# Two-layer attention trunk: layer 0's 256-column head products and layer 1's rotary ones as three float32r products, a new order of the first loads, and one place for layer 0's weight halves

## The chip, the cores and the metric

The kernel runs on one core of one Trainium2 chip. The metric is the device time of one execution in microseconds (us), the median of several runs. TensorE (PE in the profile) multiplies, PEld is its loading of stationary operands, VectorE is DVE, ScalarE is ACT, GpSimd is POOL, and SyncE (SP) issues most transfers.

## The reference

One sequence of 256 tokens with 2048 features in float32 goes through two layers. Each layer adds to x an attention and then a gated feed-forward, both behind an RMS norm. Cut to what matters:

```python
# layer 0: 16 heads of 128; with 256 tokens there is one key block, so this is causal attention
q = rope(rms_norm((h @ wq).reshape(B, S, H, dh), gq), pos, rot)      # rot = 32
k = rope(rms_norm((h @ wk).reshape(B, S, H, dh), gk), pos, rot)
v = (h @ wv).reshape(B, S, H, dh)
p = softmax(where(causal, einsum('bqhd,bhkd->bhqk', q, k) * dh ** -0.5, NEG_INF))
y = einsum('bhqk,bhkd->bqhd', p, v).reshape(B, S, H * dh) @ wo
# layer 1: low-rank q and kv; a rotary key of 64 columns is shared by the 16 heads
s = (einsum('bqhd,bkhd->bhqk', qn, k_nope) + einsum('bqhr,bkr->bhqk', qr, k_rope)) * scale
y = einsum('bhqk,bkhd->bqhd', softmax(where(causal, s, NEG_INF)), v).reshape(B, S, H * VD) @ wo
# feed-forward of each layer, 5632 wide
y = (silu(conv3(h @ w_gate) + b) * (h @ w_up)) @ w_down
```

## The kernel before, in words

**The stream of weights.** All weights pass through the core once, 370 units of up to 1 MB, cut into 1480 pieces of 128 x 512 (some 128 x 288). `Stream.load` (L72) issues a unit's transfer on SyncE's queue; three units are on their way at a time. `Stream.split` makes two float32r tiles of each piece: `whi`, a copy by ScalarE (L100), and `wlo`, the rest by VectorE (L101). It runs up to four pieces ahead of TensorE (one at the start, more by and by: `min(1 + q // 6, AHEAD_PIECES)`). A float32 product x·w becomes three float32r products: high·high, high·low, low·high.

**Two kinds of piece.** `tok_major` (L234 to L236) holds 128 tokens of h as the stationary operand and moves 512 columns of the piece: six products a piece, three for each half of the tokens. `feat_major` (L251 to L253) holds 128 columns of the piece and moves 256 tokens: twelve products a piece. Each of the two tiles of a piece has 64 spare columns, and `starts` says at which column it begins, one value for `whi` and one for `wlo`. Layer 0's q, k and v weights are units 0 to 47, twelve for each of four groups of four heads; `BY_HEADS` gives each group a place of its own, (8, 8), (8, 40), (56, 24) and (24, 56). Other token-major pieces use `BY_TOKEN` = (8, 8), feature-major ones `BY_FEATURE` = (24, 56).

**What sets the order.** The program is a list of quanta, one for a weight piece. `add` appends the products of a piece, `at(q, f)` puts other work behind quantum q, `first(q, f)` ahead of it. The last loop issues for each quantum: work put ahead, `ws.split` up to four pieces on, the products, the work behind. Each engine works strictly in the order in which its instructions were issued, and waits for others by semaphores. So the weight halves of later pieces stand on VectorE and ScalarE behind the heads' work of earlier quanta.

**The heads.** In layer 0, group g takes 48 pieces: 16 each for q, k and v. `Heads` takes q or k of four heads from PSUM (L364), sums squares (L369), asks GpSimd for the power -1/2 (L382), scales (L395), rotates (L425 to L430, through `ro1`, `ro2`), and lets TensorE transpose two heads at a time (L439); ScalarE copies the result to `qT` or `kT` (L447). `evac_values` (L549) copies v. `plan_heads` puts these at q + 0 to q + 10. A `Head` then makes the scores of 128 queries against 128 keys and of the other 128 against 256 (L463; in layer 1 a rotary product follows each, L466), masks them and takes maxima (L473), exponentiates (L482), normalises (L489, L491), transposes three blocks (L499), copies them to `pT` (L504), multiplies with v (L510 with 256 columns, L511 with 128), and splits the result into `oT` (L517 high, L518 low). All of these products are plain float32. A float32 and a float32r matmul both read f32 in the profile's rows; the line tells them apart.

**Layer 1's shared key.** `kva_turn` and `kva_rotate` prepare it, `kr_turn` (behind quantum q + 9 of the last kv piece) transposes it (L819), GpSimd clears two tiles of `room` (L823), and VectorE copies 64 rows into each (L824): the tile for even heads has the upper rows filled, the one for odd heads the lower ones.

**The way in.** TensorE runs nine products of zeros (L173). SyncE issues alternately a quarter of each of the first units (L84) and one or more of the 16 blocks of x (L177); ScalarE's queue issues the first part of `par` (L176), which holds the norm's gains. `Norm.high` (L269, ScalarE) and `Norm.low` (L274, VectorE) make a block of h, and the first piece is cast and split behind them.

Of the kernel before, what the change touches and what calls it, by code (L numbers as in the profile page):

```python
# [10 lines left out]
F32 = mybir.dt.float32  # L11
# [6 lines left out]
P = 128  # L18
# [31 lines left out]
BY_HEADS = ((8, 8), (8, 40), (56, 24), (24, 56))  # L50
# [4 lines left out]
class Stream:  # L55
# [20 lines left out]
    def begin(self, load_x):  # L76

        ends = (1, 2, 3, 4, 6, 6, 8, 8, 10, 10, 13, 16)
        at = 0
        for u in range(AHEAD_UNITS):  # L80
            src, k, n = self.units[u]
            self.raw[u] = t = self.raw_pool.tile([P, 4 * 512], F32, name="raw")
            for i in range(k):
                self.nc.sync.dma_start(t[:, i * n : (i + 1) * n], src[:, i * n : (i + 1) * n])  # L84
                end = ends[u * k + i]
                if end > at:
                    load_x(at, end)
                    at = end
        self.loaded = AHEAD_UNITS

    def split(self, upto):
        while self.split_to < min(upto, len(self.pieces)):
# [7 lines left out]
            self.nc.scalar.copy(hi[:, :n], w)  # L100
# [11 lines left out]
def trunk(ctx: ExitStack, tc: tile.TileContext, a, out):  # L112
# [39 lines left out]
    def starts(u, j):  # L152

        if u < 48:
            return BY_HEADS[u // 12]
        return BY_TOKEN if 200 <= u < 222 else BY_FEATURE
# [15 lines left out]
    for _ in range(9):  # L172
        mm(idle, zeros[:, :P], zeros, start=True, stop=True)  # L173
    warm = const.tile([P, 1], F32, name="warm")
    nc.scalar.activation(warm, ones, AF.Square)
    nc.scalar.dma_start(par[:, :C_CW], a["par"][:, :C_CW])  # L176
# [48 lines left out]
    def tok_major(state, lhs, kt, k_last, t_hi, t_lo, n):  # L225
# [4 lines left out]
        for t in range(NT):  # L230
            hi = src[:, kt, t * P : (t + 1) * P]
            lo = src[:, kt, S + t * P : S + (t + 1) * P]
            o = state["acc"][t][:, :n]
            mm(o, hi, t_hi[:, :n], start=kt == 0, stop=False)  # L234
            mm(o, hi, t_lo[:, :n], start=False, stop=False)  # L235
            mm(o, lo, t_hi[:, :n], start=False, stop=kt == k_last)  # L236
# [106 lines left out]
    class Heads:  # L343
# [22 lines left out]
        def squares(self, t):  # L366
            for i in range(self.n):
                junk = att_pool.tile([P, P], F32, name="junk", bufs=2)
# [38 lines left out]
        def rotate(self, t, stages=(0, 1)):  # L407
# [11 lines left out]
            def part(name):  # L419
                r = att_pool.tile([P, 16 * 32], F32, name=name, bufs=2)  # L420
# [30 lines left out]


    class Head:
        def __init__(self, h, qT, kT, v, i, oT, scale, rope=None):
            self.h, self.qT, self.kT, self.v, self.i = h, qT, kT, v, i
            self.oT, self.scale, self.rope = oT, scale, rope

        def scores(self):
            sc = ps_sc.tile([P, 512], F32, name="sc")
            qT, kT, i = self.qT(), self.kT(), self.i  # L460
            for q0, n, c in ((0, P, 0), (P, S, P)):
                o = sc[:, c : c + n]
                mm(o, qT[:, i, q0 : q0 + P], kT[:, i, :n], start=True, stop=self.rope is None)  # L463
                if self.rope is not None:
                    qr, kr = self.rope()
                    mm(o, qr[:, q0 : q0 + P], kr[:, :n], start=False, stop=True)  # L466
# [35 lines left out]
        def turned(self):  # L502
            self.pT = att_pool.tile([P, 3 * P], F32, name="pT", bufs=2)
            nc.scalar.copy(self.pT, self.tp[:, : 3 * P])  # L504

        def values(self):
# [3 lines left out]
            mm(o[:, :S], v[:, 0, vs], self.pT[:, :S], start=True, stop=False)  # L510
            mm(o[:, P:S], v[:, 1, vs], self.pT[:, S:], start=False, stop=True)  # L511
# [24 lines left out]
    def moba_tiles(g):  # L536
        if g == 0:
            env["oT"] = att_pool.tile([P, H, 2 * S], F32R, name="oT", bufs=1)
        env["qT", g] = att_pool.tile([P, 4, S], F32, name="qT")
        env["kT", g] = att_pool.tile([P, 4, S], F32, name="kT")  # L540
        env["v", g] = att_pool.tile([P, NT, 512], F32, name="v")
# [9 lines left out]
    def plan_heads(q, hs, key, step):  # L551
# [8 lines left out]
        for i0 in (0, 2):  # L560
            pair = {}
            at(q + step * 9 + i0 // 2, lambda hs=hs, p=pair, i0=i0, key=key: hs.turned(env[key], p, i0))
            at(q + step * 9 + i0 // 2,
               lambda hs=hs, p=pair, i0=i0, key=key: hs.turned_out(env[key], p, i0))
# [3 lines left out]
    for g in range(4):  # L568
        for kind in "qkv":
            state = {}  # L570
# [12 lines left out]
            if kind == "v":  # L583
                at(q, evac_values, state, ("v", g), lambda: n1.rstd)
                q_v = q
            else:
                hs = Heads(state, 4, P, G_Q if kind == "q" else G_K, 32, (tab, T_MC, T_MS), lambda: n1.rstd)
                plan_heads(q + (0 if g else 15 if kind == "q" else 9), hs, ("qT" if kind == "q" else "kT", g), 1)
                q_k = q
        for i in range(4):  # L590
            hd = Head(
                4 * g + i, lambda g=g: env["qT", g], lambda g=g: env["kT", g], lambda g=g: env["v", g],
                i, lambda: env["oT"], MOBA_SCALE,
# [152 lines left out]
    def open_mla():  # L746
# [7 lines left out]
        env["qrT"] = att_pool.tile([P, 8, S], F32, name="qrT", bufs=1)  # L754
# [9 lines left out]
    def kva_stats():  # L764
        ss = small.tile([P, NT, 2], F32, name="kvss")
        for t in range(NT):
            for k, (lo, hi) in enumerate(((0, 512), (512, 576))):
                junk = att_pool.tile([P, 512], F32, name="kvjunk", tag="ro1", bufs=2)
# [323 lines left out]
```

## Time and profile before

| | us |
|---|---|
| median of 3 runs | 2102.42 (2102.33 to 2102.92) |
| profiled execution | 2103.16 |
| its span, first to last instruction | 2101.3 |
| TensorE busy in the span | 2093.2 |
| VectorE busy | 1389.1 |
| ScalarE busy | 1135.1 |

Layer 0's projections and heads take the first 310 us or so of the span, layer 1's the stretch from some 1120 to 1320 us; the rest are output projections and feed-forwards.

How to read the lines of the profile that follow. A timeline row has the start and the length in us, the engine, the line of the program, the operation, output tile <- input tiles, shape, and xN for N of the same in a row; in square brackets stands how long the engine was idle ahead of it and what ended that. A row of groups has the count, then busy time in us and the mean in ns, then idle time. A row of waits has who waited, for whom, the total in us, how often, and the longest. The lengths of matmuls are modelled and overlap; the distance between starts is what counts.

### The profile page before, as it was taken

How to read it: one execution, taken by the hardware profiler on the slowest of the kernel's cores; microseconds unless marked ns; L12 is line 12 of the kernel's file. 1: busy time of each engine (PE TensorE's matmuls, PEld its weight loads, DVE VectorE, ACT ScalarE, POOL GpSimd, SP SyncE). 2: the span in 40 equal slices, each digit the busy share in tenths (PEclk: the TensorE clock that was granted, in tenths of full speed). 3: DMA queues.
4: the chain of work that ended last, by engine and by line, in shares of the span. 5: the costliest groups of instructions: out<-in, count | busy, mean ns of one | idle time of the engine just before them, and what ended most of it. 6: DMA issues, size and time to landing. Idle time of an engine off the chain costs nothing.

```text
span 2101.3 us, 42062 instructions
## 1 busy us (share of the span) xinstructions
PE 2093.2 (100%) x16683; PEld 2016.4 (96%) x16683; DVE 1389.1 (66%) x3035; ACT 1135.1 (54%) x2207; POOL 45.6 (2%) x37
## 2 busy tenths in 40 slices
PE   9999999999999999999999999999999999999999
PEld 7888889999999999999999889999999999999999
DVE  6766666766667666655555786767666667665554
ACT  6555555655555555555455675655555555544443
POOL 0000000000000000000000110000000000000000
PEclk9999999999999999999999999999999999999999
DMA  7444445555555555555554533555555555555553
GB/s 272 161 161 180 160 163 187 193 201 190 192 201 187 195 201 186 197 200 186 198 200 150 181 136 107 194 187 193 190 199 192 192 199 191 192 205 206 195 207 131
DMA packets 59381, 391.81 MB, mean 186 GB/s; under 512 B 6960, under 2 KB 10032, under 8 KB 13232
## 3 DMA queue, kind: packets, MB, share of 16 engines
q1 hardware_dynamic: 59040, 389.10, 52.1%
q8 instruction: 130, 2.13, 0.4%
q14 instruction: 67, 0.55, 0.1%
q10 hardware_dynamic: 144, 0.04, 0.0%
HBM read 387.01 MB, written 2.10 MB: 185 GB/s over the span
## 4 chain that ended last, share of the span: by engine, by line
PE 98%; DVE 1%; issue 0%; ACT 0%; POOL 0%; DMA 0%; SPq 0%; POOLq 0%; ACTq 0%
PE acc L251 26%; PE acc L253 26%; PE acc L252 26%; PE acc L235 5%; PE acc L234 5%; PE acc L236 5%; PE sc L463 1%; PE tp L439 1%; PE sc L510 1%; PE tp L499 0%; PE sc L466 0%; PE sc L511 0%; DVE wlo L101 0%; DVE junk L369 0%; POOL hr L382 0%
## 5 line engine op out<-in xcount | busy, mean ns | idle before, releaser
L101 DVE TENSOR_TENSOR wlo<-raw,whi 128x512 fp32r<-128x512 f32 (+1 forms) x1480 | 1000.8, 684 | 426.6 <-ACT whi L100 424.8
L100 ACT CAST whi<-raw 128x512 fp32r<-128x512 f32 (+1 forms) x1480 | 872.8, 614 | 463.7 <-PE acc L252 213.8
L251 PE MATMUL acc<-h,whi 128*128 128x256 f32 x2880 | 795.3, 276 | 0.0
L253 PE MATMUL acc<-h,wlo 128*128 128x256 f32 x2880 | 794.9, 276 | 0.0
L252 PE MATMUL acc<-h,whi 128*128 128x256 f32 x2880 | 794.9, 276 | 0.0
L252 PEld LDWEIGHTS acc<-h,whi 128*128 128x128 f32 x2880 | 540.7, 188 | 0.0
L251 PEld LDWEIGHTS acc<-h,whi 128*128 128x128 f32 x2880 | 540.7, 188 | 0.0
L253 PEld LDWEIGHTS acc<-h,wlo 128*128 128x128 f32 x2880 | 540.6, 188 | 0.0
L251 PE MATMUL acc<-a,whi 128*128 128x256 f32 x1408 | 388.6, 276 | 0.0
L252 PE MATMUL acc<-a,whi 128*128 128x256 f32 x1408 | 388.6, 276 | 0.0
L253 PE MATMUL acc<-a,wlo 128*128 128x256 f32 x1408 | 388.6, 276 | 0.0
L251 PEld LDWEIGHTS acc<-a,whi 128*128 128x128 f32 x1408 | 264.3, 188 | 0.0
L252 PEld LDWEIGHTS acc<-a,whi 128*128 128x128 f32 x1408 | 264.3, 188 | 0.0
L253 PEld LDWEIGHTS acc<-a,wlo 128*128 128x128 f32 x1408 | 264.3, 188 | 0.0
L234 PE MATMUL acc<-whi,h 128*128 128x512 f32 (+1 forms) x448 | 177.0, 395 | 0.7 <-ACT whi L100 0.7
L235 PE MATMUL acc<-wlo,h 128*128 128x512 f32 (+1 forms) x448 | 170.8, 381 | 0.1
L236 PE MATMUL acc<-whi,h 128*128 128x512 f32 (+1 forms) x448 | 170.2, 380 | 0.0
L251 PE MATMUL acc<-oT,whi 128*128 128x256 f32 x512 | 144.9, 283 | 0.0
L253 PE MATMUL acc<-oT,wlo 128*128 128x256 f32 x512 | 141.7, 277 | 0.0
L252 PE MATMUL acc<-oT,whi 128*128 128x256 f32 x512 | 141.6, 277 | 0.0
L665 DVE TENSOR_TENSOR g<-acc,rstd_b 128x256 f32<-128x256 f32 x88 | 37.5, 426 | 126.0 <-PE acc L253 123.0
L672 ACT ACTIVATE c<-g,par 128x256 f32<-128x256 f32 x88 | 53.1, 603 | 107.8 <-DVE g L665 107.8
(146 smaller groups left out, 1739.1 us busy)
## 6 DMA issues: line engine op xcount, KB each, us to landing
raw<-in_ffn_gu SPq DMA_DIRECT2D x176, 1024.0 KB, 4.8
raw<-in_ffn_down SPq DMA_DIRECT2D x88, 1024.0 KB, 4.8
raw<-in_moba_wk SPq DMA_DIRECT2D x16, 1024.0 KB, 4.9
raw<-in_moba_wv SPq DMA_DIRECT2D x16, 1024.0 KB, 4.8
raw<-in_moba_wo SPq DMA_DIRECT2D x16, 1024.0 KB, 4.8
raw<-in_mla_wo SPq DMA_DIRECT2D x16, 1024.0 KB, 4.8
raw<-in_moba_wq SPq DMA_DIRECT2D x13, 1024.0 KB, 4.8
raw<-in_mla_wkv_a SPq DMA_DIRECT2D x8, 576.0 KB, 3.9
```

Source lines behind the costliest of these rows:

```text
L100: self.nc.scalar.copy(hi[:, :n], w)
L101: self.nc.vector.tensor_tensor(lo[:, :n], w, hi[:, :n].bitcast(F32), op=ALU.subtract)
L234: mm(o, hi, t_hi[:, :n], start=kt == 0, stop=False)
L235: mm(o, hi, t_lo[:, :n], start=False, stop=False)
L236: mm(o, lo, t_hi[:, :n], start=False, stop=kt == k_last)
L251: mm(o, w_hi, src[:, kt, :S], start=first and k == 0, stop=False, skip_group_check=True)
L252: mm(o, w_hi, src[:, kt, S:], start=False, stop=False, skip_group_check=True)
L253: mm(o, w_lo, src[:, kt, :S], start=False, stop=kt == k_last, skip_group_check=True)
L439: nc.tensor.transpose(tp[:, (i * NT + t) * P : (i * NT + t + 1) * P], flat[:, t, c : c + P], ident)
L463: mm(o, qT[:, i, q0 : q0 + P], kT[:, i, :n], start=True, stop=self.rope is None)
L665: nc.vector.tensor_tensor(self.g[:, 2:], self.gate["acc"][:, :S], self.norm.rstd_b, op=ALU.mult)
L672: nc.scalar.activation(self.c, self.g[:, 2:], AF.Identity, bias=par[:, cb : cb + 1], scale=self.cw(2))
```

## The change

1. `Head.scores` and `Head.values` of layer 0, and the rotary part of layer 1's scores, make each product of 256 columns as three float32r products (`three`). The products of 128 columns stay float32, and so does layer 1's 256-column product of the unrotated parts.
2. For that, operands get a high and a low part. `queries_out` and `keys_out` take the place of one ScalarE copy: a float32r high part (ScalarE), a float32 copy of the first 128 columns (ScalarE), and the low part (VectorE). `evac_parts` does so for v, `Head.turned` for the transposed map. The tiles for q and k of layer 0 have one buffer instead of two. `kr_turn` writes a high and a low part and a float32 copy, and fills the other rows of the first two with zeros by VectorE.
3. `junk`, `ro1`, `ro2` and `kvjunk` have one buffer instead of two.
4. `BY_HEADS` goes: layer 0's q, k and v pieces all begin at (8, 8).
5. The way in: `par` and the first block of x go out first on SyncE's queue, the first weight quarter on ScalarE's; VectorE casts the first piece, which is split ahead of the first block of h; ten products of zeros instead of nine; the first piece's six products run in the order high·high for both token halves, then high·low, then low·high.

```diff
-BY_HEADS = ((8, 8), (8, 40), (56, 24), (24, 56))
...
-        ends = (1, 2, 3, 4, 6, 6, 8, 8, 10, 10, 13, 16)
-        at = 0
+        ends = (2, 2, 3, 4, 6, 6, 8, 8, 10, 10, 13, 16)
+        load_x(0, 1)
+        at = 1
...
-                self.nc.sync.dma_start(t[:, i * n : (i + 1) * n], src[:, i * n : (i + 1) * n])
+                queue = self.nc.scalar if u == i == 0 else self.nc.sync
+                queue.dma_start(t[:, i * n : (i + 1) * n], src[:, i * n : (i + 1) * n])
...
-            self.nc.scalar.copy(hi[:, :n], w)
+            if i == 0:
+                self.nc.vector.tensor_copy(hi[:, :n], w)
+            else:
+                self.nc.scalar.copy(hi[:, :n], w)
...
-        if u < 48:
-            return BY_HEADS[u // 12]
-        return BY_TOKEN if 200 <= u < 222 else BY_FEATURE
+        return BY_TOKEN if u < 48 or 200 <= u < 222 else BY_FEATURE
...
-    for _ in range(9):
+    for _ in range(10):
...
-    nc.scalar.dma_start(par[:, :C_CW], a["par"][:, :C_CW])
+    nc.sync.dma_start(par[:, :C_CW], a["par"][:, :C_CW])
...
+        if state.get("first") and kt == 0:
+            order = [(t, part) for part in range(3) for t in range(NT)]
+        else:
+            order = [(t, part) for t in range(NT) for part in range(3)]
...
+    def three(o, w_hi, w_lo, m_hi, m_lo, start, stop):
+        mm(o, w_hi, m_hi, start=start, stop=False)
+        mm(o, w_hi, m_lo, start=False, stop=False)
+        mm(o, w_lo, m_hi, start=False, stop=stop)
...
+            if self.parts:
+                (q0, q1), (k0, k) = qT, kT
+                mm(sc[:, :P], q0[:, i], k0[:, i], start=True, stop=True)
+                three(sc[:, P : 3 * P], q1[:, 0, i], q1[:, 1, i], k[:, 0, i], k[:, 1, i], True, True)
+            else:
+                qr0, qr1, kr0, kr = self.rope()
+                mm(sc[:, :P], qT[:, i, :P], kT[:, i, :P], start=True, stop=False)
+                mm(sc[:, :P], qr0, kr0, start=False, stop=True)
+                mm(sc[:, P : 3 * P], qT[:, i, P:], kT[:, i], start=True, stop=False)
+                three(sc[:, P : 3 * P], qr1[:, 0], qr1[:, 1], kr[:, 0], kr[:, 1], False, True)
...
+            nc.scalar.copy(hi, self.tp[:, :S])
+            nc.scalar.copy(self.pT1, self.tp[:, S : 3 * P])
+            nc.vector.tensor_tensor(lo, self.tp[:, :S], hi.bitcast(F32), op=ALU.subtract)
...
+                three(o[:, :S], v0[:, 0, vs], v0[:, 1, vs], self.pT[:, 0], self.pT[:, 1], True, False)
+                mm(o[:, P:S], v1[:, vs], self.pT1, start=False, stop=True)
...
+    def keys_out(dst, tp, i0):
+        k0, k = dst
+        src = tp.rearrange("p (a s) -> p a s", a=2)
+        hi, lo = k[:, 0, i0 : i0 + 2], k[:, 1, i0 : i0 + 2]
+        nc.scalar.copy(hi, src)
+        nc.scalar.copy(k0[:, i0 : i0 + 2], src[:, :, :P])
+        nc.vector.tensor_tensor(lo, src, hi.bitcast(F32), op=ALU.subtract)
...
         for i in range(2):
-            nc.gpsimd.memset(env["kr"][i], 0.0)
-            nc.vector.tensor_copy(env["kr"][i][i * 64 : (i + 1) * 64, :], tp[i * 64 : (i + 1) * 64, :S])
+            rows, rest = (slice(j * 64, (j + 1) * 64) for j in (i, 1 - i))
+            hi, lo = env["kr"][:, i, 0], env["kr"][:, i, 1]
+            nc.gpsimd.memset(env["kr0"][:, i], 0.0)
+            for t in (hi, lo):
+                nc.vector.tensor_copy(t[rest], zeros[rest, :S])
+            nc.vector.tensor_copy(hi[rows], tp[rows, :S])
+            nc.vector.tensor_tensor(lo[rows], tp[rows, :S], hi[rows].bitcast(F32), op=ALU.subtract)
+            nc.vector.tensor_copy(env["kr0"][rows, i], tp[rows, :P])
...
+    ws.split(1)
     for f, args in side.pop(-1):
```

`queries_out` is `keys_out` with the token halves the other way round (the high and low parts of the second 128 queries, a float32 copy of the first), and `evac_parts` splits v's first 128 tokens and copies the rest.

110 lines of the change are left out of this document (73 added, 37 removed).

## The prediction

> **What bounds the kernel now.** First the page: shares of the engines and the chain that ended last.
>
> ```profile
> PE 2093.2 (100%) x16683; PEld 2016.4 (96%) x16683; DVE 1389.1 (66%) x3035; ACT 1135.1 (54%) x2207; POOL 45.6 (2%) x37
> PE 98%; DVE 1%; issue 0%; ACT 0%; POOL 0%; DMA 0%; SPq 0%; POOLq 0%; ACTq 0%
> ```
>
> TensorE is 98% of that chain, so a nanosecond taken from one of its products is a nanosecond off the span, and work on another engine counts only where TensorE then waits. Where it does, the view of who waited for whom says; asked for TensorE's matmul row from 60 to 330 us (layer 0's heads; one line is the whole answer) and from 1130 to 1340 us (layer 1's heads).
>
> ```profile
> PE tp L439 <- DVE qk L430: 0.4, 1, 0.4
> ...
> PE acc L235 <- DVE wlo L101: 0.8, 1, 0.8
> ```
>
> Layer 0 has one wait of 0.4 us. The line from layer 1, where a weight piece's low half comes late from VectorE, stands at a place that the change touches.
>
> **The change, part by part. (1) Products of 256 columns.** The groups by line and shape give the counts, the timeline the starts. A busy time of a matmul is modelled and overlaps the next, so I use the distance from one start to the next.
>
> ```profile
> L463 PE MATMUL sc<-kT,qT 128*128 128x256 f32 x32 | 9.6, 380 | 0.0
> L510 PE MATMUL sc<-pT,v 128*128 128x256 f32 x32 | 9.5, 378 | 0.0
> L466 PE MATMUL sc<-room,qrT 128*128 128x256 f32 x32 | 9.5, 379 | 0.0
> ...
> 94.27 0.59 PE L510 MATMUL sc<-pT,v 128*128 128x256 f32 x2
> 94.70 0.38 PE L511 MATMUL sc<-pT,v 128*128 128x128 f32 x2
> ...
> 1202.63 0.60 PE L463 MATMUL sc<-room 128*128 128x256 f32 x2
> 1203.07 0.59 PE L466 MATMUL sc<-room,qrT 128*128 128x256 f32 x2
> ...
> 499.78 0.28 PE L252 MATMUL acc<-h,whi 128*128 128x256 f32 x1
> ...
> 500.46 0.28 PE L252 MATMUL acc<-h,whi 128*128 128x256 f32 x1
> ```
>
> A full float32 product leaves two records, so the 32 records of each of the first three rows are 16 products, 48 in all. One takes 94.70 - 94.27 = 0.43 us, or 1203.07 - 1202.63 = 0.44. A float32r product of 256 columns takes (500.46 - 499.78) / 6 = 0.113 us in the feed-forward (the second start is the sixth after the first), three of them 0.34. There the two operands lie at other places than the heads' tiles will; layer 0's 512-column float32r products, quoted in part 2, start 0.227 apart or, at another place, 0.233; half of these are 0.113 and 0.117. I take 0.116, that is 0.348 for three against 0.435: 0.087 saved, times 48 = **4.2 us saved**. Ends: at 0.113, 4.6; at 0.122, twice the spread above it, 3.3. The 128-column products stay float32 and cost what they did.
>
> **(2) One place for layer 0's heads.** A weight piece is six products of 512 columns, so the starts of L234 six products apart give a piece. Here are pieces with nothing put between, one each from groups 0, 1, 2 and 3.
>
> ```profile
> 53.64 0.39 PE L234 MATMUL acc<-whi,h 128*128 128x512 f32 x1
> ...
> 55.00 0.39 PE L234 MATMUL acc<-whi,h 128*128 128x512 f32 x1
> ...
> 131.52 0.40 PE L234 MATMUL acc<-whi,h 128*128 128x512 f32 x1
> ...
> 132.92 0.40 PE L234 MATMUL acc<-whi,h 128*128 128x512 f32 x1
> ...
> 198.27 0.40 PE L234 MATMUL acc<-whi,h 128*128 128x512 f32 x1
> ...
> 199.66 0.39 PE L234 MATMUL acc<-whi,h 128*128 128x512 f32 x1
> ...
> 273.06 0.39 PE L234 MATMUL acc<-whi,h 128*128 128x512 f32 x1
> ...
> 274.44 0.39 PE L234 MATMUL acc<-whi,h 128*128 128x512 f32 x1
> ```
>
> Group 0, which lies where all four will lie, needs 1.36 us; groups 1, 2 and 3 need 1.40, 1.39 and 1.38. VectorE and ScalarE do the same kind of work beside all of them (squares of heads in each), so the place is what differs. The tiles that these products read keep their addresses in the change. Pieces next to transposes or a head's products are irregular in every group and I count no gain there: by the planned places that leaves about 20 quiet pieces of 48 in group 1 and 27 each in groups 2 and 3. 20 x 0.04 + 27 x 0.03 + 27 x 0.02 = 2.15; the rounding of the starts leaves 1.2 to 2.6. **2.0 us saved.**
>
> **(3) The way in.**
>
> ```profile
> 1.19 4.02 PE L173 MATMUL sc<-zeros 128*128 128x512 bf16 x9 [1.19 <-DVE zeros L170]
> 4.81 0.51 ACT L269 ACTIVATE h<-xT,par 128x256 fp32r<-128x256 f32 x1 [2.58 <-DMA xT<-in_xT]
> 5.22 0.60 ACT L100 CAST whi<-raw 128x512 fp32r<-128x512 f32 x1
> 5.86 0.69 DVE L101 TENSOR_TENSOR wlo<-raw,whi 128x512 fp32r<-128x512 f32 x1
> 5.88 0.79 PE L234 MATMUL acc<-whi,h 128*128 128x512 f32 x1 [0.67 <-ACT whi L100]
> 6.61 0.79 PE L235 MATMUL acc<-wlo,h 128*128 128x512 f32 x1
> ...
> 9.18 0.69 DVE L101 TENSOR_TENSOR wlo<-raw,whi 128x512 fp32r<-128x512 f32 x1
> ...
> 9.76 0.63 PE L236 MATMUL acc<-whi,h 128*128 128x512 f32 x1
> 10.18 0.46 PE L234 MATMUL acc<-whi,h 128*128 128x512 f32 x1
> ...
> 10.95 0.40 PE L234 MATMUL acc<-whi,h 128*128 128x512 f32 x1
> ...
> 5.00:10.00 5.00, 4.33 (x10) 1.00 0.98 307
> ```
>
> ScalarE makes h and then the weight's high half, one after the other, and TensorE, out of warm-up products, waits for the second until 5.88; then again for the low half. In the change VectorE casts the first piece while ScalarE makes h. The x transfer goes out second on SyncE's queue as before (the parameters take the weight's place ahead of it, and the weight theirs on ScalarE's queue), so I leave h at 4.81 to 5.32. The weight, issued with the first transfers as before, should come with x, at 4.8; VectorE's cast takes at most what its subtraction of that width takes, 0.69, so the high half is ready by 5.5 and the low half by 6.2. The ten warm-up products end at 1.19 + 10 x 0.427 = 5.46, and the first real one follows them. Its new order (both high-high products, then both high-low) needs the low half only at 6.3, so the gap at 6.6 goes too.
>
> Until about 10.2 a product takes 10.18 - 9.76 = 0.42 (0.427 over the stretch), and 0.227 later. TensorE's clock is slow at first, though the granted clock in the last row above (TensorE's busy time with its count, clock, share of the DMA engines, GB/s) reads 1.00 for 5 to 10 us. If the slow time still ends at 10.2, (10.18 - 5.46) / 0.427 = 11 products stand before that point instead of 9: two of 0.227, 0.46 saved. But the slow time held for 3.6 us of unbroken products from 6.6 on; with nothing broken since 1.19 it probably ends earlier, and an end at 8.6 already puts five more products ahead: 1.2. The third piece bounds it: its low half is ready at 9.18 + 0.69 = 9.87, transfers of x setting that pace, and TensorE uses it at 10.95 + 0.23, so no more than 1.3 can be had. **1.2 us saved**, ends 0.4 and 1.3. The Trainium skill, "TensorE: Matmul & The Clock Gate", Part 1, says that the array is throttled by default and is released at the end of a whole busy window of about 3.4 us that runs free of the kernel. By that rule the window that ended at 10.2 was the first whole one, and the one that ended at 6.8 was broken by the gap ahead of 5.88; unbroken, it would end the slow time at 6.8 and save the full 1.3. The trace agrees as far as one end of a slow stretch can show it.
>
> **(4) The shared rotary key of layer 1.** Here the change costs. In `kr_turn`, two copies by VectorE become ten operations.
>
> ```profile
> L491 DVE TENSOR_SCALAR s<-s,sst 128x256 f32<-128x256 f32 x32 | 11.1, 348 | 0.0
> L518 DVE TENSOR_TENSOR oT<-sc,oT 128x256 fp32r<-128x256 f32 x32 | 13.6, 424 | 27.0 <-ACT oT L517 27.0
> ...
> 1187.58 0.86 DVE L824 COPY room<-tp 64x256 f32<-64x256 f32 x2 [1.18 <-POOL room L823]
> ...
> 1189.91 0.69 DVE L101 TENSOR_TENSOR wlo<-raw,whi 128x512 fp32r<-128x512 f32 x1
> ...
> 1190.65 0.50 PE L235 MATMUL acc<-wlo,cqT 128*128 128x512 f32 x1 [0.81 <-DVE wlo L101]
> ```
>
> VectorE is free from 1187.58 - 1.18 = 1186.40 but waits for GpSimd's memset; the two copies then take 0.86, and a low half at 1189.91 ends just before the product that waited 0.81 for it. After the change VectorE starts at 1186.40 with copies of zeros, which wait for nothing. Two zero copies (0.35 by L491, of which some 0.08 overlaps the next, as three low halves of 0.69 take 1.89 in part 5: 0.27), the high part 0.43 as in L824, the low part 0.42 as in L518, and an estimated 0.29 for the copy of 128 columns, a third under L824's: 1.68, twice 3.36, to 1189.76, where it was 1188.44 before. TensorE waits at that very point, so **1.3 us is lost**. Zero copies at 0.10 or at the 0.43 of L824 make 0.6 to 1.9.
>
> **(5) What lies beside TensorE.** Layer 0 gives VectorE a low part for every q and k pair, for v and for each head's turned map: per group 2 x 0.42 + 2 x 0.69 + 0.69 + 4 x 0.42 = 4.6 us of some 70 (0.42 by L518, 0.69 by L101), and ScalarE a second, smaller copy beside each. VectorE is at 66% and runs four pieces (5.4 us) ahead of TensorE.
>
> ```profile
> L504 ACT COPY pT<-tp 128x384 f32<-128x384 f32 x32 | 15.3, 479 | 5.0 <-PE tp L499 4.9
> ...
> 140.51 1.89 DVE L101 TENSOR_TENSOR wlo<-raw,whi 128x512 fp32r<-128x512 f32 x3
> 143.10 0.69 DVE L101 TENSOR_TENSOR wlo<-raw,whi 128x512 fp32r<-128x512 f32 x1 [0.69 <-ACT whi L100]
> ```
>
> Even after a group's heaviest stretch it idles again within three low halves. A new low part waits for three transposes (0.33, an estimate) and ScalarE's copy (under the 0.48 of L504), with its own 0.42 some 1.2 us, with weight halves behind it that are wanted three pieces (4.1 us) later: hidden. Where that cover is thinnest, at the 0.4 us wait of group 0, ScalarE's extra copy adds some 0.2; ends 0 and 0.6. The single buffers for q, k, junk and the rotary parts are rewritten only after their last reader by the plan, or by the same engine: nothing. Layer 1's low parts of rotary queries (four of 0.42) fall where VectorE is ahead: nothing, 0.4 if not.
>
> **Sum:** -4.2 - 2.0 - 1.2 + 1.3 + 0.2 = **-5.9 us.** The profiled execution took 2103.16 (span 2101.3, 1.9 around it), which gives 2097.3. It lies 0.7 above the median of the three runs, 2102.42, in which the change is to be seen: **2096.5**.
>
> **The rivals.** *The place does not carry over:* the locked pace of group 0 belongs to its quiet, and with heads at work all groups run at 1.40. Part 2 turns into a loss of some 0.8 in groups 2 and 3: 2099.3. Against it: group 0's pieces with squares beside them keep 1.36. *Three products cost what one did:* with both operands of the heads' products at one place each takes 0.145 instead of 0.116: no gain in part 1, 2100.7. Against it, 512 columns take 0.227 at that same place. *VectorE holds TensorE up* (slower than before): it works in order, and every one of layer 0's 16 heads now makes it wait in mid-queue for TensorE and ScalarE. If its lead there were under about 1.8 us (1.2 of waiting and a low half of 0.60), TensorE would wait some 1.1 us a head: 17.6 - 5.9 = 11.7 lost, 2114.1. Against it: no such wait in the view today, though low parts of the heads' outputs already wait in the same way. *The slow clock ends when it did:* 2097.2, inside the forecast.
>
> **How the numbers follow.** Forecast with either end of the slow clock 0.82; place 0.07; products 0.05; VectorE 0.06. The forecast's own terms reach from -4.6 - 2.6 - 1.3 + 0.6 = -7.9 to -3.3 - 1.2 - 0.4 + 1.9 + 1.0 = -2.0, not all at once; I state 2094.5 to 2100.2, which takes in the rival of the place. A run can tell about 0.2%, 4.2 us, from no change: faster means below 2098.2. Of the forecast's 0.82, 0.75 lies there and 0.07 above; the place gives 0.02 and 0.05; the products 0.05 to no change; VectorE 0.06 to slower. Faster 0.77, same 0.17, slower 0.06.
>
> **What would show it.** Right: the heads' three products start 0.113 to 0.12 apart; pieces of groups 1 to 3 with nothing between take 1.36; the first real product starts near 5.5 and fast ones well before 10.2; the wait for the low half near 1190 us grows from 0.8 to some 2.1 us. Wrong: VectorE's low halves as the releaser of waits in layer 0, pieces of 1.38 or more in groups 1 to 3, or another lasting wait in layer 1.

## The result and the profile after

The changed kernel takes **2107.35 us** (median of 11 runs, 2106.47 to 2108.44); the kernel before took 2102.92 beside it (11 runs, 2102.16 to 2103.77). The ratio is 1.0021 (95% interval 1.0012 to 1.0029): 4.4 us slower, where 2096.5 was forecast. The span of the profiled execution is 2105.5 us, 4.2 over that of before.

The page after, busy shares and the chain that ended last:

```profile
PE 2089.8 (99%) x16732; PEld 2013.4 (96%) x16732; DVE 1418.3 (67%) x3084; ACT 1137.8 (54%) x2242; POOL 45.3 (2%) x37
PE 92%; DVE 5%; ACT 1%; issue 1%; DMA 1%; POOL 1%; SPq 0%; ACTq 0%; POOLq 0%
```

TensorE is busy 3.4 us less, so products and place did act. But its share of the chain fell from 98 to 92%, and VectorE's rose from 1 to 5%: the end now runs through VectorE at many places. Who waited for whom on TensorE, first from 60 to 330 us (layer 0's heads), then from 1130 to 1340 us (layer 1's):

```profile
PE tp L449 <- DVE qk L440: 0.9, 2, 0.4
PE acc L235 <- DVE wlo L105: 0.5, 1, 0.5
```

```profile
PE acc L235 <- DVE wlo L105: 5.1, 5, 2.3
PE tp L885 <- DVE ckv L862: 1.4, 2, 1.2
PE tp L898 <- DVE krr L880: 1.1, 2, 0.7
```

Each kernel has line numbers of its own: L449 is the transpose of q and k (L439 before), L105 the low half (L101), L885 and L898 the transposes of layer 1's compressed values and of its shared key (L806 and L819). In layer 1 one wait of 0.8 for a low half has become five of 5.1 together, and not only at `kr_turn`.

To see where the time went, I set the start of each weight piece's first product beside the same piece of before. After minus before, in us, with the time in the kernel before: +0.56 at piece 18 (33 us), +1.30 at 40 (64 us), +2.07 at 50 (79 us), then falling through layer 0 to -0.72 at piece 204 (325 us), flat through the feed-forward, -0.72 still at 809, then up to +4.8 at 878 (1251 us), from where layer 1's heads bring it down to the +4.2 of the end. So the products and the place did gain, and three stretches took it back: the first pieces, group 0's first heads, and layer 1's preparation (a fourth, within groups 1 to 3, shows only beside an experiment). The trace says by what. VectorE sums squares in between, and here is the first set of them, before (L369) and after (L379):

```profile
53.37 0.28 DVE L369 CUSTOM_DVE_ANT_0 junk<-qk 128x128 f32<-128x128 f32 x1
53.59 0.08 DVE L369 DVE_READ_ACCUMULATOR2_ANT ss<- 128x1 f32 x1
53.59 0.28 DVE L369 CUSTOM_DVE_ANT_0 junk<-qk 128x128 f32<-128x128 f32 x1
...
54.01 0.28 DVE L369 CUSTOM_DVE_ANT_0 junk<-qk 128x128 f32<-128x128 f32 x1
```

```profile
53.94 0.29 DVE L379 CUSTOM_DVE_ANT_0 junk<-qk 128x128 f32<-128x128 f32 x1
54.15 0.08 DVE L379 DVE_READ_ACCUMULATOR2_ANT ss<- 128x1 f32 x1
54.27 0.29 DVE L379 CUSTOM_DVE_ANT_0 junk<-qk 128x128 f32<-128x128 f32 x1
...
54.94 0.29 DVE L379 CUSTOM_DVE_ANT_0 junk<-qk 128x128 f32<-128x128 f32 x1
```

Before, a square starts with the reading of the last one's accumulator: 0.21 us from start to start. After, 0.12 us pass between the reading's start and the next square: 0.33 us. In the program as built, each square now waits on VectorE's own semaphore until the square just before it has written `junk`; with two buffers it waits for the one before that, which is long done. The reading of the accumulator belongs to the square: the next one starts 0.04 us after the reading's end (54.15 + 0.08 against 54.27). There are 160 squares, in runs of four to eight, so some 120 such gaps, about 14 us of VectorE's time. 128 of the 160 are those of q and k (`junk<-qk`), which TensorE wants next.

The rows that answer to the other steps. The three products of 256 columns (L464 to L466) start 0.11 to 0.12 apart, as forecast, except that in the scores the first stands 0.20 ahead of the second; one set of scores and of values:

```profile
84.46 0.36 PE L464 MATMUL sc<-k,q 128*128 128x256 f32 x1
84.66 0.28 PE L465 MATMUL sc<-k,q 128*128 128x256 f32 x1
84.78 0.28 PE L466 MATMUL sc<-k,q 128*128 128x256 f32 x1
84.90 0.40 PE L235 MATMUL acc<-whi,h 128*128 128x512 f32 x1
...
95.97 0.28 PE L464 MATMUL sc<-pT,v 128*128 128x256 f32 x1
96.08 0.28 PE L465 MATMUL sc<-pT,v 128*128 128x256 f32 x1
96.20 0.28 PE L466 MATMUL sc<-pT,v 128*128 128x256 f32 x1
```

Pieces of groups 1, 2 and 3 with nothing between (the products with the low half stand three apart, so twice the distance is a piece): 0.68, 1.36 a piece in all three.

```profile
127.15 0.39 PE L235 MATMUL acc<-wlo,h 128*128 128x512 f32 x1
...
127.83 0.39 PE L235 MATMUL acc<-wlo,h 128*128 128x512 f32 x1
...
198.10 0.39 PE L235 MATMUL acc<-wlo,h 128*128 128x512 f32 x1
...
198.78 0.39 PE L235 MATMUL acc<-wlo,h 128*128 128x512 f32 x1
...
274.47 0.39 PE L235 MATMUL acc<-wlo,h 128*128 128x512 f32 x1
...
275.15 0.39 PE L235 MATMUL acc<-wlo,h 128*128 128x512 f32 x1
```

The way in: the first real product starts at 5.25, products stand 0.23 apart from 5.84 on (a row with x2 or x3 holds two or three), and then TensorE waits, for the second piece's low half and the third piece's high half, behind x's third block at 8.37.

```profile
5.25 0.75 PE L235 MATMUL acc<-whi,h 128*128 128x512 f32 x2
5.84 0.63 PE L235 MATMUL acc<-wlo,h 128*128 128x512 f32 x2
6.30 1.02 PE L235 MATMUL acc<-whi,h 128*128 128x512 f32 x3
...
7.54 0.50 PE L235 MATMUL acc<-wlo,h 128*128 128x512 f32 x1 [0.22 <-DVE wlo L105]
...
8.37 0.51 ACT L279 ACTIVATE h<-xT,par 128x256 fp32r<-128x256 f32 x1 [1.60 <-DMA xT<-in_xT]
...
9.44 0.50 PE L235 MATMUL acc<-whi,h 128*128 128x512 f32 x1 [0.47 <-ACT whi L104]
```

### The profile page after: what moved, and what is told of

Same layout as the page of the kernel before. It is cut to its first block, busy times and chain, and to the rows that moved or that the text cites. A ratio compares the mean times of both kernels' runs of the same rounds, so it can differ in the third digit from the quotient of the medians.

```text
span 2105.5 us, 42253 instructions
## 1 busy us (share of the span) xinstructions
PE 2089.8 (99%) x16732; PEld 2013.4 (96%) x16732; DVE 1418.3 (67%) x3084; ACT 1137.8 (54%) x2242; POOL 45.3 (2%) x37
## 4 chain that ended last, share of the span: by engine, by line
PE 92%; DVE 5%; ACT 1%; issue 1%; DMA 1%; POOL 1%; SPq 0%; ACTq 0%; POOLq 0%
PE acc L263 26%; PE acc L261 26%; PE acc L262 26%; PE acc L235 11%; DVE wlo L105 1%; DVE junk L379 1%; DVE qk L405 1%; PE tp L449 1%; POOL hr L392 1%; PE tp L520 0%; ACT whi L104 0%; DMA raw<-in_moba_wq 0%; ACT qk L374 0%; PE sc L545 0%; DMA xT<-in_xT 0%
## 5 line engine op out<-in xcount | busy, mean ns | idle before, releaser
L105 DVE TENSOR_TENSOR wlo<-raw,whi 128x512 fp32r<-128x512 f32 (+1 forms) x1480 | 1000.3, 684 | 402.1 <-ACT whi L104 399.2
L235 PE MATMUL acc<-whi,h 128*128 128x512 f32 (+1 forms) x896 | 277.4, 382 | 0.5 <-ACT whi L104 0.5
L235 PEld LDWEIGHTS acc<-whi,h 128*128 128x128 f32 x896 | 164.7, 188 | 30.9 <-ACT whi L104 1.4
```

Of the source, the lines that this page charges most:

```text
L105: self.nc.vector.tensor_tensor(lo[:, :n], w, hi[:, :n].bitcast(F32), op=ALU.subtract)
L235: mm(state["acc"][t][:, :n], src[:, kt, c : c + P], (t_lo if part == 1 else t_hi)[:, :n], start=kt == 0 and part == 0, stop=kt == k_last a ...
```

## The experiments

The theory: the single buffer of `junk` holds VectorE up, and VectorE's lead at q, k and the low halves behind them was thin. The rival: VectorE's new low parts and `kr_turn` hold it up. Medians below are over 6 to 11 runs unless said, each beside the kernel before on the same chip (2102.63 to 2103.00).

| kernel | median, us | ratio to before, 95% interval |
|---|---|---|
| a_junk2 | 2098.95 | 0.9981 (0.9972 to 0.9990) |
| b_junk1 | 2109.75 | 1.0032 (1.0020 to 1.0044) |
| a_oldway_j2 | 2098.14 | 0.9978 (0.9969 to 0.9987) |
| b_wayin | 2103.14 | 1.0000 (0.9991 to 1.0009) |
| b_place | 2100.34 | 0.9988 (0.9979 to 0.9997) |
| best | 2096.61 | 0.9971 (0.9960 to 0.9981) |
| b_halfx | 2102.04 | 0.9997 (0.9988 to 1.0006) |
| b_way_halfx | 2102.23 | 0.9997 (0.9988 to 1.0006) |
| b_way_dma | 2103.17 | 1.0002 (0.9993 to 1.0011) |
| b_way_comp | 2103.00 | 0.9999 (0.9990 to 1.0008) |
| best_comp | 2096.53 | 0.9970 (0.9958 to 0.9981) |
| b_ro1 | 2103.32 | 1.0002 (0.9993 to 1.0011) |
| a_products | 2100.92 | 0.9993 (0.9984 to 1.0001) |
| a_junk2_look (1 run) | 2098.29 | |
| b_u3 | 2102.38 | 0.9999 (0.9990 to 1.0008) |
| best_comp_u3 | 2096.38 | 0.9969 (0.9958 to 0.9981) |

### The one buffer

**a_junk2**, the changed kernel with this edit, and **b_junk1**, the kernel before with its reverse:

```diff
-                junk = att_pool.tile([P, P], F32, name="junk", bufs=1)
+                junk = att_pool.tile([P, P], F32, name="junk", bufs=2)
```

> The changed kernel with two buffers for the squares' output (junk) instead of one; nothing else differs. Theory A, the single buffer: the accumulating squares on VectorE now start 0.33 us apart instead of 0.21, so every set of heads leaves VectorE 0.4 to 1.6 us later, and TensorE waits for it at the transposes of the keys and at the low halves near 135, 1147, 1150 and 1253 us. With two buffers the pitch is 0.21 again and most of these waits go: about 5 us less than the changed kernel, 2102.4 (2100.5 to 2104). Theory B, the added work itself (low parts on VectorE, second copies on ScalarE, ten operations in kr_turn): the pitch returns to 0.21 but the waits stay, since VectorE's added operations cause them: 2106 to 2107.4. If the pitch stays at 0.33, the buffer is not what sets it.

> The kernel before with one buffer for the squares' output instead of two; nothing else differs. Theory A: the pitch of the squares goes from 0.21 to 0.33 us, and as VectorE was just in time at the transposes of the keys, at the two low halves behind layer 1's first rotary set and at the shared rotary key, TensorE waits there: 3 to 5 us more than before, 2105.5 to 2108. Theory B: VectorE has slack without the added work and absorbs the gaps: within 0.7 us of before.

Measured: 2098.95, which is **8.4 us under the changed kernel**, and 2109.75, 6.8 us over before; both lie beyond the ranges that I gave, on the side of theory A. This one digit is the whole loss and more. (In six of the eleven runs of a_junk2 the mean granted clock is a little under full, for which see the last section; the median of the other five is 2097.83.) The groups of squares, changed kernel first, then a_junk2 (busy and mean, then idle ahead):

```profile
L379 DVE CUSTOM_DVE_ANT_0 junk<-qk 128x128 f32<-128x128 f32 x128 | 37.1, 290 | 3.3
```

```profile
L379 DVE CUSTOM_DVE_ANT_0 junk<-qk 128x128 f32<-128x128 f32 x128 | 29.5, 286 | 0.0
```

And TensorE's waits in layer 1 in a_junk2; from 60 to 330 us only the 0.4 for L440 is left, as before the change:

```profile
PE acc L235 <- DVE wlo L105: 1.9, 1, 1.9
PE tp L885 <- DVE ckv L862: 1.4, 2, 1.2
PE tp L898 <- DVE krr L880: 0.3, 1, 0.3
```

The rival falls as the cause of the loss: with all the added low parts in place, layer 0 has no wait that it did not have. What is left of it is `kr_turn`, the wait of 1.9 us (below). The loss is larger in the changed kernel (8.4) than in the one before (6.8). The piece starts show where: groups 1 to 3 give 2.3 us between a_junk2 and the changed kernel and 0.9 between before and b_junk1. The low parts alone cost nothing there; that they use up slack in which the gaps could have hidden fits, but was not tried by itself.

**b_ro1** tests the other single buffers (`ro1`, `ro2`, and `kvjunk`, which shares the place of `ro1`) in the kernel before:

```diff
-                r = att_pool.tile([P, 16 * 32], F32, name=name, bufs=2)
+                r = att_pool.tile([P, 16 * 32], F32, name=name, bufs=1)
-                junk = att_pool.tile([P, 512], F32, name="kvjunk", tag="ro1", bufs=2)
+                junk = att_pool.tile([P, 512], F32, name="kvjunk", tag="ro1", bufs=1)
```

> The kernel before with one buffer for the rotary parts and the squares of layer 1's compressed values (which share their place), and two for junk as before. The prediction put this at nothing. The trace of the kernel with two junk buffers still has a step of 0.45 us near 1176 us, where TensorE waits for the compressed values, and none at the rotary steps: 0.3 to 0.6 above before, 2103.3. Rival: the single rotary parts hold VectorE up as the squares do, in every set of heads: 1.5 or more above before.

Measured: 0.36 over before, inside the interval of no change. The piece starts show one step of 0.37 us near 1176 us, where TensorE's wait for the compressed values (`ckv`) grows, and nothing at the rotations, where other instructions stand between a buffer's last reader and its next writer. That wait, before and in b_ro1:

```profile
PE tp L806 <- DVE ckv L783: 1.0, 2, 0.8
```

```profile
PE tp L806 <- DVE ckv L783: 1.3, 2, 1.1
```

### The place and the products

**b_place**, the kernel before with this edit alone:

```diff
-        if u < 48:
-            return BY_HEADS[u // 12]
-        return BY_TOKEN if 200 <= u < 222 else BY_FEATURE
+        return BY_TOKEN if u < 48 or 200 <= u < 222 else BY_FEATURE
```

> The kernel before with one place for layer 0's heads alone. As predicted, the quiet pieces of groups 1 to 3 fall to 1.36 us: 2.0 us saved (1.2 to 2.6), 2101.0. The trace with two buffers gives 5.1 us for layer 0 together, of which the products' measured 0.154 us a head times 16 make 2.5, so that the place would be the upper end, 2.6: 2100.4. Rival: the two do not add (the place helps only beside the new products): within 0.5 of before.

Measured: 2100.34, 2.5 us saved. **a_products** is a_oldway_j2 (below) with that edit undone, so that of the three gains only the products are left:

> The changed kernel with two buffers for the squares' output, the old way in and the old four places of layer 0's heads: the new products alone are left, with kr_turn and the single rotary buffers that came with them. If the terms add: products 3.6 us by the traces' 78, 76 and 72 ns a head and stage, less 1.1 for kr_turn and 0.4 for the rotary buffers, 2.1 below before, 2100.8 (2100.3 to 2101.3). If the place carries part of the products' gain (layer 0's operands at one place), less than 1.5 below before.

Measured: 2100.92, 1.7 us under before (2102.63), within the range expected, though its interval just takes in no change. Its piece starts gain 2.55 us in layer 0's heads and 1.3 in layer 1's. From the product ahead of a head's products to the second one behind them, the changed kernel needs 79 ns less than before in layer 0's scores, 79 in its values and 74 in layer 1's scores (means over the heads), 16 x 232 = 3.7 us. Place and products add: -2.5 and -1.7 make -4.2, and a_oldway_j2, which has both, stands 4.9 under before.

### The shared rotary key

**best** is the changed kernel with two `junk` buffers, the old way in, and a lighter `kr_turn` (the added lines stand in `open_mla`):

```diff
-            nc.gpsimd.memset(env["kr0"][:, i], 0.0)
-            for t in (hi, lo):
-                nc.vector.tensor_copy(t[rest], zeros[rest, :S])
...
-            nc.vector.tensor_copy(env["kr0"][rows, i], tp[rows, :P])
+            nc.scalar.copy(env["kr0"][rows, i], tp[rows, :P])
...
+        nc.gpsimd.memset(env["kr0"], 0.0)
+        for i in range(2):
+            for t in range(2):
+                nc.gpsimd.tensor_copy(env["kr"][(1 - i) * 64 : (2 - i) * 64, i, t], zeros[(1 - i) * 64 : (2 - i) * 64, :S])
```

> The changed kernel with two buffers for the squares' output, the old way in, and a lighter kr_turn: the four zero copies and the memset go to GpSimd at the opening of layer 1's tiles, the copies of 128 columns to ScalarE; VectorE keeps four operations. Theory: the wait of TensorE near 1187 us (start to start 2.28 us in both kernels with two buffers) follows from kr_turn's 3.1 us on VectorE; with some 1.6 us there the wait falls to about 0.8 us, and 1.5 us go: near 2096.6 (2096.0 to 2097.6). Rival: the wait has another cause, the squares and low parts behind kr_turn, and stays: 2098.1.

Measured: **2096.61**, 1.5 under a_oldway_j2, of which the piece starts put 1.1 at this place. TensorE's wait for the low half, first in a_oldway_j2, then here:

```profile
PE acc L232 <- DVE wlo L100: 1.9, 1, 1.9
```

```profile
PE acc L232 <- DVE wlo L100: 0.7, 1, 0.7
```

This version beats both kernels, by 6.2 us the one before and by 10.7 the changed one.

### The way in

**b_wayin** is the kernel before with the change's hunks in `begin`, `split` and `tok_major`, the tenth warm-up product and `ws.split(1)`; **a_oldway_j2** is a_junk2 with those hunks undone. **b_way_dma** has only the first diff below, **b_way_comp** the rest of the hunks without it, and **best_comp** is the version best with those of b_way_comp.

```diff
-        ends = (1, 2, 3, 4, 6, 6, 8, 8, 10, 10, 13, 16)
-        at = 0
+        ends = (2, 2, 3, 4, 6, 6, 8, 8, 10, 10, 13, 16)
+        load_x(0, 1)
+        at = 1
...
+                queue = self.nc.scalar if u == i == 0 else self.nc.sync
...
-    nc.scalar.dma_start(par[:, :C_CW], a["par"][:, :C_CW])
+    nc.sync.dma_start(par[:, :C_CW], a["par"][:, :C_CW])
```

> The kernel before with the new way into the kernel alone: the order of the first transfers and their queues, VectorE's cast of the first piece, ten warm-up products, the first piece's product order, its split ahead of the heads of h. The trace of the changed kernel has its 19th and later pieces start 0.56 us later than before. Theory A: that belongs to the way in, whose early gain of 2.1 us is lost again to transfers that land some 0.85 us later: 2103.5, 0.3 to 0.9 above before. Rival, as predicted: the way in gains some 1.2 us by itself and something else in the changed kernel takes it: 2101.7.

> The changed kernel with two buffers for the squares' output and the way in of the kernel before. If the two costs are separate and simply add, it stands 0.3 to 0.9 below the changed kernel with two buffers alone: near 2101.8. If the later transfers are caught up elsewhere, the same as that kernel. It would be the first version below the kernel before: products and place give 5.6 us, and layer 1's shared rotary key takes 1 to 2 of them, so that 2098 to 2102 is what this theory can bear.

> The kernel before with the new order of the first transfers and their queues alone (parameters and x first on SyncE's queue, the first weight on ScalarE's); products, casts and warm-up as before. Theory: this part is what takes the way in's gain back: the third row of x is issued at 3.65 to 3.9 us instead of 3.06, the DMA engines are at 80 to 86% from 5 to 7.5 us instead of 92 to 99%, and TensorE waits at pieces 2 to 4 and 11 to 13. 0.3 to 1.0 above before: 2103.4. Rival: the order of transfers costs nothing and the gain is lost to the kernel's compute side: 2102.5 to 2103.

> The kernel before with the compute side of the new way in alone: VectorE's cast of the first piece, ten warm-up products, the first piece's order of products, its split ahead of the heads of h; transfers and queues as before. Theory: without the later issues the early start is kept in part: 0.3 to 1.2 below before, 2102.1. Rival: within 0.2 of before, since x's rows 2 to 4 set these pieces whatever stands ahead of them.

> The lighter version (two buffers, lighter kr_turn) with the compute side of the new way in and the old transfers. If the theory of the transfers holds, it stands 0.3 to 1.2 below that version with the old way in, 2095.9; if not, at 2096.6 or above.

Measured: +0.1 for the whole in the kernel before, neither the 0.3 to 0.9 lost that I expected nor the 1.2 gained of the rival, +0.2 and 0.0 for its halves, and best_comp 0.1 under best: none is clear of no change. a_oldway_j2 is 0.8 below a_junk2, but that is not shown to be the way in: without the runs whose mean granted clock is under full (last section), six of a_junk2's and three of a_oldway_j2's, the medians are 2098.08 for a_oldway_j2 and 2097.83 for a_junk2. My theory that the order of the transfers takes the gain back falls: undoing that order gains nothing. **b_halfx** and **b_way_halfx** (the old way in and the new) take x's second half off the first 20 us; both leave it out of h, whose second half they make from x's first:

```diff
-    ws.begin(lambda j0, j1: nc.sync.dma_start(xT[:, j0:j1, :], a["xT"][:, j0:j1, :]))
+    ws.begin(lambda j0, j1: j0 < 8 and nc.sync.dma_start(xT[:, j0:j1, :], a["xT"][:, j0:j1, :]))
...
-            nc.scalar.activation(self.h[:, j, :S], xT[:, j, :], AF.Copy, scale=g)
+            nc.scalar.activation(self.h[:, j, :S], xT[:, j % self.cut, :], AF.Copy, scale=g)
...
+    n1.cut = 8
+    at(14, lambda: nc.sync.dma_start(xT[:, 8:, :], a["xT"][:, 8:, :]))
```

> The kernel before with half of x's transfer (1 MB) taken from the start to piece 14; the second half of h is made from the first half of x, the rest is computed as before. It takes away supply load from the first 20 us. Theory: transfers bound the first 13 pieces, so unit 3 of the weights, which the cast waited for until 22.5 us, lands 2 to 3 us earlier, and the kernel gains what TensorE waited there, 0.5 to 1.2 us. Rival: ScalarE or VectorE paces these pieces: no gain.

> The same with the new way in. Theory: the way in brings TensorE 2 us ahead by piece 1 and loses it to the transfers; with the load taken away most of it stays, so that this kernel stands 1.0 to 1.9 us below the previous one from piece 18 on. Rival: the new way in loses its gain to something that it does itself (ScalarE's order, the first products' order): the same time as the previous kernel within 0.4.

Measured: b_halfx 0.8 under before, b_way_halfx 0.2 over b_halfx, neither clear of no change. So less load may help a little, which is not shown, and the new way in still gives nothing. **b_u3** and **best_comp_u3** (on before and on best_comp) send the fourth unit in quarters:

```diff
-            self.nc.sync.dma_start(t[:, : k * n], src)
+            for i in range(4 if u == 3 else 1):
+                m = k * n // (4 if u == 3 else 1)
+                self.nc.sync.dma_start(t[:, i * m : (i + 1) * m], src[:, i * m : (i + 1) * m])
```

> The kernel before with the fourth unit of weights (1 MB) sent in four transfers of 256 KB instead of one; the way in as before. Theory: its first quarter lands 1 to 3 us earlier, and the waits at pieces 11 to 14 that half of the traces show go: 0.2 to 0.8 below before, 2102.4. Rival: the landing of that unit is not what sets piece 18: no change.

> The lighter version with the compute side of the new way in and the fourth unit in four transfers. Theory: with that landing out of the way, the early start is kept: 0.4 to 1.2 below the lighter version, 2095.8. Rival: no change, 2096.5.

Measured: 0.25 under before and 0.15 under best_comp, neither clear of no change. The fourth unit's first cast comes earlier in the one trace of b_u3 than in the one of before; here before, then b_u3:

```profile
22.54 0.62 ACT L100 CAST whi<-raw 128x512 fp32r<-128x512 f32 x1 [2.42 <-DMA raw<-in_moba_wq]
```

```profile
20.11 0.62 ACT L102 CAST whi<-raw 128x512 fp32r<-128x512 f32 x1 [0.64 <-PE acc L238]
```

Neither kernel has the waits at pieces 11 to 14 that ten other traces show; but before and some others lack them too, and here two earlier pieces take 1.9 us each instead of 1.36 (2 and 3 in b_u3, 3 and 4 in best_comp_u3). In the sixteen traces with all of x loaded at the start, piece 1 starts anywhere from 6.8 to 8.9 us and piece 18 between 31.7 and 33.3, with neither way in clearly earlier. In the two traces with half of x it starts at 31.4 and 31.9. That the supply of the first 4 MB of weights and 2 MB of x sets that point fits the waits for transfers; it is not shown, since 1 MB less moves the point by so little. Which landing is the last differs from one execution to the next, and I have not settled what moves it.

### One stretch of slow clock

**a_junk2_look** is a_junk2 once more.

> The changed kernel with two buffers for the squares' output once more, for a second trace of the stretch from 1185 to 1192 us. If the slow stretch depends on where the clock's windows lie against the wait, this trace may have it or not, with the wait the same 2.28 us, and its span is 2096.5 to 2098.2 accordingly. If the kernel itself sets it, the stretch is there again at the same place.

Measured: the same wait, and no slow stretch; its rows stand in the last section.

## Why the prediction was wrong

**Part 5 failed, by one sentence:** that single buffers rewritten "by the same engine" cost nothing. I took an engine that works in order to be free of waiting for itself. In this program it isn't: the rewrite waits on a semaphore until the earlier write is complete, 0.12 us at each square. The single buffers stood at nothing in a part of +0.2, and measured +8.4 for `junk` and about +0.4 for `kvjunk`. The rest of part 5 held: the low parts in layer 0 cost nothing (a_junk2), not even the 0.2 that I gave ScalarE's copy in group 0.

The Trainium skill, "VectorE: DVE Perf Modes", section "The DRAIN you can't avoid", says of eight chained copies that a semaphore after each took as long as one after the last, 13.88 us, and that it "costs nothing extra here". The squares here differ: 0.33 us from start to start with the wait, 0.21 without; for them the measurement decides.

**Part 3 failed too**: -1.2 forecast, +0.1 measured, which is not clear of nothing. The early start came (5.25; fast from 5.84), and a gain at piece 1 with it. Two things were wrong. First, I bounded it by the third piece alone, but engines wait for landings behind it, up to the fourth unit's; what takes the gain back stays open. Second, the slow products up to 10.2 us were not the kernel's but that one execution's. In b_place, with the way in of before, they are already fast at 6.6, and piece 1 starts at 7.49 instead of 8.90:

```profile
5.50 0.50 PE L232 MATMUL acc<-whi,h 128*128 128x512 f32 x1 [0.29 <-ACT whi L100]
...
6.56 0.39 PE L234 MATMUL acc<-whi,h 128*128 128x512 f32 x1
...
7.49 0.39 PE L232 MATMUL acc<-whi,h 128*128 128x512 f32 x1
```

All eight traces with the old way in other than that of before look like this one (piece 1 at 7.5 to 7.8), so of the 2.1 us by which piece 1 leads in the changed kernel some 1.3 belong to the profiled execution of before. Nor is the rest certain: in b_wayin piece 1 starts at 7.65. The Trainium skill, "TensorE: Matmul & The Clock Gate", Part 1, says that the clock's window runs free of the kernel, so that the moment of release varies; I used its length and not this consequence, which the traces bear out: the slow products end at 10.2 us in one of the nine traces and by 6.8 in the others.

**Part 1 held, a little large:** 3.7 against 4.2 forecast, as three products save 74 to 79 ns and not 87. **Part 2 held:** 2.5 against 2.0, and 1.36 us a piece as said. **Part 4 held:** in a_oldway_j2, where the squares have two buffers, TensorE's wait grows from 0.8 to 1.9 (forecast 2.1), 1.1 us against 1.3; `kr_turn` takes VectorE 3.1 us instead of 3.36, as here in the changed kernel from its first copy to what follows the last:

```profile
1188.59 0.49 DVE L906 CAST kr<-zeros 64x256 fp32r<-64x256 bf16 x2
...
1191.70 0.69 DVE L397 TENSOR_TENSOR qk<-qk,hr 128x512 f32<-128x512 f32 x1
```

The sum with the measured terms: -3.7 - 2.5 + 0.1 + 1.1 + 0.4 + 8.4 = +3.8, against +4.4 measured. Of the signs that I had named for being wrong, VectorE's low halves as the releaser of a wait in layer 0 and lasting waits in layer 1 both came.

**The rivals.** That the place does not carry over, and that three products cost what one did, are refuted; so is that the slow clock ends when it did. The rival on the slower side named the right engine and the wrong cause: it had VectorE wait in mid-queue for TensorE and ScalarE at every head, and those waits cost nothing. What it did have right is that VectorE's lead can be too thin: at q and k it is, and there the gaps ate it.

## What to carry to other kernels

Where a program orders its buffers by semaphores, as this one does, an engine that writes the same scratch tile twice in a row waits for itself. Give even a result that nobody reads a second buffer, and when a buffer count goes down, look at how many instructions stand between two writes to that buffer. Look for such gaps not where the engine is busiest but where its result is wanted next. And before you price a short stretch of one profiled execution, ask whether the stretch is the kernel's or that execution's: with the same way in, this kernel's second piece starts up to 1.4 us earlier in one execution than in another, and that says little about where its start-up ends: b_junk1 is 1.2 us ahead of before at the second piece and 0.3 behind it at the 19th.

## What the runs showed of the hardware

After a pause TensorE can run on at half its clock, so that the pause costs more than itself. In a_junk2 TensorE waits for a low half from 1184.98 to 1187.27 us, runs on at 0.23 us a product, and from 1188.33 at 0.43 for 3.4 us. Its rows, and the windows of 3.4 us around them (TensorE's busy time with its count, further engines, granted clock, share of the DMA engines, GB/s):

```profile
1184.98 0.39 PE L235 MATMUL acc<-whi,cqT 128*128 128x512 f32 x1
1187.27 0.50 PE L235 MATMUL acc<-wlo,cqT 128*128 128x512 f32 x1 [1.89 <-DVE wlo L105]
...
1188.33 0.63 PE L235 MATMUL acc<-whi,cqT 128*128 128x512 f32 x1
```

```profile
1184.90:1188.30 3.40, 1.51 (x7) 0.91 (x6) 3.39 (x17) 1.30 (x3) 0.00 (x0) 0.99 0.32 135
1188.30:1191.70 3.40, 3.40 (x11) 2.73 (x10) 2.48 (x9) 1.19 (x2) 1.94 (x1) 0.51 0.14 19
```

The second execution of the same kernel, over the same work:

```profile
1184.60:1188.00 3.40, 1.51 (x7) 0.94 (x6) 3.39 (x17) 1.33 (x3) 0.00 (x0) 1.00 0.34 140
1188.00:1191.40 3.40, 3.40 (x19) 2.65 (x18) 2.48 (x9) 1.64 (x3) 1.94 (x1) 1.00 0.05 10
```

The granted clock is 0.51 in the one and 1.00 in the other; eleven matmuls run where nineteen do, and the piece behind starts 1.35 us later. In the traces of a_oldway_j2 and a_products the same wait (2.29 and 2.30 from start to start) passes at full clock, and so does the one in the changed kernel, 2.65. So it is not the length alone; that the place of the clock's window against the wait decides fits, but was not tried. The Trainium skill, "TensorE: Matmul & The Clock Gate", section "Why this matters for your kernels", advises against idle gaps of over about 3 us; here one of 2.28 from start to start was followed by half clock in one trace of the four that have it.

How often it comes, the granted clock of every run shows. 3.4 us at half clock out of 2100 bring a run's mean from 1.000 to 0.999. In the three kernels with the wait of 2.3 us it reads 0.999 in six, three and five of eleven runs each (a_junk2, a_oldway_j2, a_products), and in each of the three these are the slowest: in a_junk2 2098.95 to 2100.47, against 2097.63 to 2098.58 for the five at 1.000. In the changed kernel, with 2.65 us, it reads 0.999 in two of eleven. In the others, where TensorE's longest gap behind the start-up is at most 1.6 us from start to start in the traces, every run reads 1.000, among them all 107 of the kernel before that stand beside the experiments. A mean does not say where a stretch lies; but a clock under full comes and goes with the execution, and only kernels with the long wait show it.
